# Second feed-forward product by seven block products, in one layer of a streaming encoder on one Trainium2 core

## The chip, the cores and the metric

The kernel runs on one core of a Trainium2 chip. Its engines work side by side: TensorE (PE, with its weight loads shown apart as PEld), VectorE (DVE), ScalarE (ACT), GpSimd (POOL) and SyncE (SP), whose queue issues nearly all DMAs here. The metric is the device time of one execution in microseconds; three runs of the kernel before gave 1771.66, 1764.99 and 1768.73 us, median 1768.73. Everything below about durations is from one profiled execution of it.

## The reference

One layer of a hybrid encoder for 1024 prompt rows and 64 sample rows (1088 columns in the kernel, which holds everything transposed). Projections, sparse attention, a pooling mixer and cross-attention come first and are not touched. The end of the layer is what matters:

```python
def merge_and_ffn(x, ..., w_gate, w_up, w_down):
    ...                                   # x, h = rmsnorm(x, g_ffn)
    return x + (jax.nn.silu(h @ w_gate) * (h @ w_up)) @ w_down
# D_MODEL = 1024, D_FF = 2816 = 22 blocks of 128 rows
```

All of it is in float32. The kernel makes a float32 product from three products of fp32r numbers: each operand is split into a high part (a cast) and a low part (the operand less its high part), and hi x hi, hi x lo and lo x hi are added in PSUM. In what follows "lo" is that second part, computed by one subtraction on VectorE (helper `lo_of`, line 86 of both kernels).

## The kernel before

**Order of the work.** A scheduler orders the instructions of each engine from the program's order and the tiles' dependencies; tiles come from pools with a fixed number of buffers, and an instruction waits until the buffer that it writes has been read for the last time. SP issues DMAs in its own order, so that a DMA whose buffer isn't free holds back those behind it. With `tc.issue_after(x)` a DMA is placed behind x in that order.

**Hidden layer.** The 1088 columns are two sets, 512 and 576 columns (`SETS`), and each is cut into halves of 256 or 288. The 22 row blocks of the hidden layer are worked as 11 pairs p of two blocks. `pair_product` computes one pair for w_gate or w_up: the weights (two loads of 512 KB, L1103) and the normed input are seen as 2 x 2 blocks, and the 2 x 2 product is made from seven block products instead of eight (Strassen-Winograd). For that, sums of weight blocks (`ws`, L1110, three on VectorE, one on GpSimd for each call) and sums of the results (L1141) are needed. Each of the seven has 4 k-blocks x 3 terms of 128x256 or 128x288 products per set (L1127). Weights are cast on ACT (L1119) into a tile of two (`split_tiles`, two buffers) and their lo part is made on VectorE.

`hidden(p, sets)` calls it for w_gate and w_up and then forms u = silu(gate) * up in the tile `tg` (L1186 to L1200), which is stored to DRAM as `u_d[p]` (two blocks of 1088 columns). Pairs 0 and 1 get their first set from `direct` by plain products while the second set's input is still being normed, and only the second set from `hidden`; pairs 2 to 10 get both sets.

**Down stage.** The columns are cut into three chunks (364, 362 and 362). For each chunk eight PSUM banks collect, over the 22 row blocks, 8 output blocks x 3 terms of 128x364 or 128x362 (L1275): 3 x 22 x 24 = 1584 products. For each row block the chunk of u (`uf`, L1266) and 512 KB of w_down (`raw2`, through `wblock`, L110) are loaded, cast on ACT and given lo parts on VectorE, four buffers deep. Then the residual y is added from `yt` (L1279), and the sum is stored (L1280).

Of the kernel before, what the change touches and what calls it, by code (L numbers as in the profile page):

```python
# [45 lines left out]
def encoder_step(ctx: ExitStack, tc: tile.TileContext, a: dict, o: list):  # L46
# [30 lines left out]
    def mm(dt=F32):  # L77
        return psum[0].tile([128, 512], dt, name="mm", tag="mm", bufs=n_mm[0])
# [1017 lines left out]

    def pair_product(name, p, sets, outs, finish):
        raws = []  # L1100
        for e in range(2):
            raw = raw_tile() if (name == "w_up") == (p >= EARLY) else fa.tile([128, 1024], F32, name="fr", tag="fr", bufs=2)
            SP.dma_start(raw.rearrange("p (k j) -> p k j", k=KT), a[name][p + e * NP])  # L1103
# [49 lines left out]
        product(chain, a22, 3, False, True, lambda i: finish(i, t21[i], chain[i]))  # L1153


    def direct(p, between={}):
        n = SETS[0][1]
        h = n // 2
        blocks = [[(HH[0][0][q], HH[0][1][q]) if q is not None else b12_hl for q in qs] for qs in ((0, 1), (None, 2))]
        g = fu.tile([128, 2, n], F32, name="tg", tag="tg", bufs=2)  # L1160
        for name in ("w_gate", "w_up"):
            for e in range(2):
                if (name, e) in between:
                    between[name, e]()
                w = wblock(a[name][p + e * NP], (KT, 128))
                for c in range(2):
                    ps = mm()[:, :h]
                    matmul3(ps, [(w[0][:, k], w[1][:, k], blocks[c][k // 4][0][:, k % 4], blocks[c][k // 4][1][:, k % 4])
                                 for k in range(KT)])
# [5 lines left out]
                if name == "w_up":  # L1175
                    SP.dma_start(u_d[p][e, :, :n], g[:, e])

    def hidden(p, sets):
        def out(i, nm, bufs):
# [10 lines left out]
        pair_product("w_gate", p, sets, g, gate_last)  # L1190
        v = {i: out(i, "tu", 1) for i in sets}

        def up_last(i, t, ps):
            t0, n = SETS[i]
# [7 lines left out]
        pair_product("w_up", p, sets, v, up_last)  # L1202

    EARLY = 2
    turn2, pair_w = [0], []
    u_d = [dram.tile([2, 128, T], F32, name=f"u{p}") for p in range(NP)]
    sq0 = out_proj(0)
    mix_c[1].__exit__(None, None, None)
    hp0_c = tc.tile_pool(name="h0", bufs=1)
# [3 lines left out]

    b12_c = tc.tile_pool(name="b12", bufs=1)
    b12_p = b12_c.__enter__()
    b12_hl = [b12_p.tile([128, 4, 256], F32R, name=f"b12{nm}") for nm in "hl"]

    def first_sums():
        rb = norm_rows(0, *st.pop())
# [32 lines left out]


    fu_c.__exit__(None, None, None)
    for c in (hp1_c, b12_c, fa_c, hp0_c):
        c.__exit__(None, None, None)
    late_c = tc.tile_pool(name="late", bufs=1)
    late = late_c.__enter__()
    for c0, cn in CH:
        acc = [mm()[:, :cn] for f in range(KT)]  # L1260
        for kb in range(NF):
            p, e = kb // 2, kb % 2
            first_kb = c0 == 0 and kb < 2
            up_, nb = (dn, 2) if first_kb else (late, 4)
            uf = up_.tile([128, 364], F32, name="uf", tag="uf", bufs=nb)[:, :cn]
            SP.dma_start(uf, u_d[p][e, :, c0:c0 + cn])  # L1266
            wh, wlo = wblock(a["w_down"][kb], (KT, 128), *(() if first_kb else (
                late.tile([128, 1024], F32, name="raw2", tag="raw2", bufs=4),
                [late.tile([128, 1024], F32R, name=nm, tag=nm, bufs=4) for nm in ("wh2", "wl2")])))
            uh, ul = [up_.tile([128, 364], F32R, name=nm, tag=nm, bufs=nb)[:, :cn] for nm in ("uh", "ul")]  # L1270
            A.copy(uh, uf)
            lo_of(ul, uf, uh)
# [3 lines left out]
        for f in range(KT):  # L1276
            yt = late.tile([128, 364], F32, name="yt", tag="yt", bufs=12)[:, :cn]
            SP.dma_start(yt, y_d[f, :, c0:c0 + cn])
            V.tensor_tensor(yt, acc[f], yt, op=OP.add)  # L1279
            SP.dma_start(o[0][f, :, c0:c0 + cn], yt)  # L1280
    for c in (late_c, dn_c):
        c.__exit__(None, None, None)

# [64 lines left out]
```

## Time and profile before

| what | value |
|---|---|
| median of three runs | 1768.73 us (1764.99 to 1771.66) |
| the profiled execution's own time | 1774.77 us |
| its span | 1772.7 us |
| mean granted clock of TensorE | 0.993 of full speed |
| TensorE busy | 1719.6 us, 97% of the span, 11810 products |
| VectorE, ScalarE, GpSimd busy | 63%, 46%, 23% |
| DMA over the span | 224.26 MB, 127 GB/s |
| hidden layer's products (L1127), idle time before them | 3 x 1120 records, 1.1 us |
| down stage's products (L1275), idle time before them | 3 x 512 records, 0.0 us |

Read the page from its top: which engine is busy nearly all the time, then in which slices, then which lines cost most there and what ended the idle time before them. The duration printed for a product is modelled and contains its pipelining; what one product costs in a stream is read from how many start in a window. A few records of products are missing in the groups of the page, so the counts of the program (1584, for one) are used.

### The profile page before, as it was taken

The numbers are of one execution on the slowest core, as the hardware profiler recorded it, in microseconds if no ns is written. First come the engines' busy times: TensorE is split into PE (matmuls) and PEld (weight loads), VectorE is DVE, ScalarE is ACT, GpSimd is POOL, SyncE is SP. The second block draws the span as 40 slices with busy tenths as digits, with TensorE's granted clock in tenths as the row PEclk, the third lists the DMA queues.
The fourth block names the chain that finished last, engine by engine and source line by source line (L and its number), as shares of the span: only waits on it lengthen the run. The fifth ranks groups of instructions, "written<-read, shape, count | busy, mean of one in ns | idle before, by whom it ended". The sixth has DMA issues, their size and how long they took to land.

```text
span 1772.7 us, 31533 instructions
## 1 busy us (share of the span) xinstructions
PE 1719.6 (97%) x11810; PEld 1668.6 (94%) x11810; DVE 1124.5 (63%) x2411; ACT 813.6 (46%) x1927; POOL 409.5 (23%) x444
## 2 busy tenths in 40 slices
PE   6999999999999998989899999999999999999999
PEld 6999999999999998877798999999999999999999
DVE  6567999999954433778783887544444454544443
ACT  5456677737523432569631354433333333433332
POOL 4111414355412213765203432110000000000000
PEclk9999999999999998999999999999999999999999
DMA  7222441232475336650354333222222221867673
GB/s 231 61 67 73 161 130 46 78 90 98 118 200 190 104 99 207 194 158 1 130 209 137 111 115 130 85 74 74 74 76 89 79 74 43 312 185 244 184 229 98
DMA packets 128582, 224.26 MB, mean 127 GB/s; under 512 B 23463, under 2 KB 86303, under 8 KB 128430
## 3 DMA queue, kind: packets, MB, share of 16 engines
q1 hardware_dynamic: 128430, 222.26, 39.0%
q8 instruction: 93, 1.52, 0.4%
q14 instruction: 59, 0.48, 0.1%
HBM read 167.84 MB, written 54.37 MB: 125 GB/s over the span
## 4 chain that ended last, share of the span: by engine, by line
PE 76%; DVE 11%; ACT 3%; issue 3%; DMA 3%; POOL 2%; SPq 0%; DVEq 0%; ACTq 0%; POOLq 0%
PE mm L1127 24%; PE mm L120 17%; PE mm L1275 15%; PE fl L120 13%; DVE junk_v L780 2%; ACT junk_a L777 2%; PE acc L933 1%; PE tr L903 1%; PE mm L333 1%; DVE wlo L86 1%; PE mm L926 1%; DMA gt<-side_m 1%; DVE lo L86 1%; DVE pl L86 1%; DVE tmlo L86 1%
## 5 line engine op out<-in xcount | busy, mean ns | idle before, releaser
L1127 PE MATMUL mm<-hi,whi 128*128 128x288 f32 (+1 forms) x1120 | 323.2, 289 | 1.1 <-DVE tu L1141 1.1
L1127 PE MATMUL mm<-hi,wlo 128*128 128x288 f32 (+1 forms) x1120 | 324.2, 290 | 0.0
L1127 PE MATMUL mm<-lo,whi 128*128 128x288 f32 (+1 forms) x1120 | 323.5, 289 | 0.0
L1127 PEld LDWEIGHTS mm<-hi,whi 128*128 128x128 f32 x1120 | 211.8, 189 | 1.8 <-DVE tu L1141 1.6
L1127 PEld LDWEIGHTS mm<-lo,whi 128*128 128x128 f32 x1120 | 211.8, 189 | 0.0
L1127 PEld LDWEIGHTS mm<-hi,wlo 128*128 128x128 f32 x1120 | 211.2, 189 | 0.4 <-DVE wlo L86 0.4
L120 PE MATMUL fl<-hh,whi 128*128 128x362 f32 (+1 forms) x576 | 189.7, 330 | 0.9 <-ACT hh L133 0.9
L120 PE MATMUL fl<-hl,whi 128*128 128x362 f32 (+1 forms) x576 | 189.8, 330 | 0.0
L120 PE MATMUL fl<-hh,wlo 128*128 128x362 f32 (+1 forms) x576 | 189.6, 330 | 0.0
L1275 PE MATMUL mm<-uh,wh 128*128 128x362 f32 (+1 forms) x512 | 167.4, 328 | 0.0
L1275 PE MATMUL mm<-ul,wh 128*128 128x362 f32 (+1 forms) x512 | 166.8, 326 | 0.0
L1275 PE MATMUL mm<-uh,wl 128*128 128x362 f32 (+1 forms) x512 | 166.0, 326 | 0.0
L86 DVE TENSOR_TENSOR wl<-raw,wh 128x1024 fp32r<-128x1024 f32 x64 | 78.4, 1225 | 123.4 <-ACT wh L94 123.3
L94 ACT CAST wh<-raw 128x1024 fp32r<-128x1024 f32 x64 | 67.3, 1051 | 145.6 <-PE mm L1275 137.5
L120 PE MATMUL mm<-tmlo,hh 128*128 128x256 f32 (+3 forms) x432 | 122.9, 286 | 1.5 <-DVE tmlo L86 1.5
L120 PE MATMUL mm<-tmhi,hh 128*128 128x256 f32 (+3 forms) x432 | 122.1, 288 | 2.0 <-POOL tmhi L96 2.0
L120 PE MATMUL mm<-tmhi,hl 128*128 128x256 f32 (+3 forms) x432 | 122.6, 286 | 0.0
L86 DVE TENSOR_TENSOR wlo<-raw,whi 128x1024 fp32r<-128x1024 f32 (+1 forms) x75 | 75.9, 1022 | 63.4 <-ACT whi L1119 37.5
L777 ACT ACTIVATE junk_a<-score,cand_a,sgn_a 128x512 f16<-128x512 f32 (+2 forms) x93 | 95.5, 1027 | 42.1 <-DVE cand_a L794 21.8
L120 PEld LDWEIGHTS fl<-hh,whi 128*128 128x128 f32 x576 | 108.3, 188 | 1.7 <-POOL rs L125 1.1
L120 PEld LDWEIGHTS fl<-hl,whi 128*128 128x128 f32 x576 | 108.2, 188 | 0.6
L120 PEld LDWEIGHTS fl<-hh,wlo 128*128 128x128 f32 x576 | 108.2, 188 | 0.5
(386 smaller groups left out, 4545.1 us busy)
## 6 DMA issues: line engine op xcount, KB each, us to landing
raw<-in_w_down_dram SPq DMA_DIRECT2D x66, 512.0 KB, 3.8
fraw<-in_w_gates_dram SPq DMA_DIRECT2D x24, 512.0 KB, 3.7
raw<-in_w_up_dram SPq DMA_DIRECT2D x22, 512.0 KB, 3.8
fr<-in_w_gate_dram SPq DMA_DIRECT2D x18, 512.0 KB, 3.7
side<-side_a SPq DMA_DIRECT2D x8, 1088.0 KB, 6.3
raw<-in_w_out_dram SPq DMA_DIRECT2D x16, 512.0 KB, 3.7
uf<-u SPq DMA_DIRECT2D x44, 181.0 KB, 3.7
u<-tg SPq DMA_DIRECT2D x22, 288.0 KB, 2.1
```

Of the source, the lines that this page charges most:

```text
L86: V.tensor_tensor(lo, src, hi.bitcast(F32), op=OP.subtract)
L94: A.copy(hi, src)
L120: PE.matmul(ps, l, r, start=i == 0, stop=i == n - 1)
L333: PE.matmul(ps[:n, :cn], qt[:, h, :n], kstack[:, k0 + c:k0 + c + cn], start=True, stop=True)
L777: A.activation(junk[:n, :nk], sc, AF.Sign, bias=bj, scale=1.0 if scale is None else scale[:n, j:j + 1], accum_out=sj)
L780: V.tensor_scalar(junk[:n, :nk], sc, bj, None, op0=OP.is_ge, op1=OP.add, accum_out=sj)
L903: PE.matmul(lg[:n, i * 512:i * 512 + cn], qT[:, h, :n], kT[:, kv, s, k0 + c:k0 + c + cn], start=s == 0, stop=s == 1)
L926: PE.transpose(pt[:cn, i * n:(i + 1) * n], probs[i][:, c:c + cn], ident[:n, :n])
L933: PE.matmul(acc, vv, r, start=ji == 0 and i == 0, stop=ji == nj - 1 and i == 1)
L1127: PE.matmul(dst[i], l, r, start=start and j == 0, stop=stop and j == 11, skip_group_check=True)
L1275: PE.matmul(acc[f], l, r, start=kb == 0 and j == 0, stop=kb == NF - 1 and j == 2)
```

## The change

The down product too is now made from seven block products. u of a pair is a row of two blocks, and each of its two column sets has two halves; so u is a 2 x 2 of blocks, and w_down, two row blocks by two halves of the 1024 outputs, another.

- `keep_u` makes the four sums of u that are needed (four subtractions on VectorE per set, L1162), in the tile `tu` of the up product, which is no longer needed then, and stores seven half blocks per pair (L1165 to L1167), 128 x 544 each for both sets. In `hidden` these stores are not issued at once but collected in `later` and issued in the next pair, behind its w_gate loads.
- `down_load` reads a pair's two w_down blocks (2 x 512 KB, L1176), placed behind the w_gate load of a later pair (`SUMS_AT`: pairs 0 and 1 during pair 2, 4 and 5 during pair 5, the others one by one during pairs 3 to 10). `down_sums` makes four sums of 128x512 in place on VectorE (L1181 to L1184), `down_store` stores them (L1188) for products 6, 4, 2 and 5; products 0, 1 and 3 use w_down as it is.
- The down stage runs products 4, 2, 1, 0, 5, 6, 3. Each has 11 blocks (one per pair) of 4 output blocks x 2 column sets x 3 terms of 128x256 and 128x288 (L1343): 7 x 11 x 24 = 1848 products. A block loads 128 x 544 of u and 128 x 512 of weights, eight buffers deep. After a product its eight banks are added into the tile `yl` (L1358), which holds the whole residual and is loaded in 32 parts between the blocks' loads (L1381); after products 0, 5, 6 and 3 the results are stored (L1360). Products 4 and 2 add up in the same banks, and so do products 0, 5, 6 and 3; the list in the diff says which starts or ends a bank. In the last product the blocks of pairs 3 to 10 are held and go bank by bank.

```diff
@@ pair_product
+            ld = SP.dma_start(raw.rearrange("p (k j) -> p k j", k=KT), a[name][p + e * NP])
+        if loaded:
+            loaded(ld.ins)
...
+    def keep_u(i, p, u, t):
+        c0, c1 = UC[i], UC[i + 1]
+        b11, b12, b21, b22 = u[:, 0, 0], u[:, 0, 1], u[:, 1, 0], u[:, 1, 1]
+        for q, x, y_ in ((4, b12, b11), (5, b22, t[:, 1]), (6, b22, b12), (3, b21, t[:, 2])):
+            V.tensor_tensor(t[:, q - 3], x, y_, op=OP.subtract)
+        def store():
+            SP.dma_start(u_d[p][0, :, c0:c1], b11)
+            SP.dma_start(u_d[p][1:3, :, c0:c1].rearrange("q p t -> p q t"), u[:, 1])
+            SP.dma_start(u_d[p][3:7, :, c0:c1].rearrange("q p t -> p q t"), t)
+        return store
+    def down_load(p):
+        pool, tag, n = ((dn, "ud", T), (b12_p, "b12", 1024))[p % 2 == 0]
+        rs = [pool.tile([128, n], F32, name="dr", tag=tag, bufs=2)[:, :1024] for e in range(2)]
+        for e, r in enumerate(rs):
+            SP.dma_start(r.rearrange("p (f j) -> p f j", f=KT), a["w_down"][2 * p + e])
+        return rs
+    def down_sums(r0, r1):
+        a11, a21, a12, a22 = r0[:, :512], r0[:, 512:], r1[:, :512], r1[:, 512:]
+        V.tensor_tensor(a11, a11, a21, op=OP.subtract)
+        V.tensor_tensor(a21, a21, a22, op=OP.add)
+        V.tensor_tensor(a22, a22, a11, op=OP.subtract)
+        V.tensor_tensor(a12, a12, a22, op=OP.subtract)
@@ hidden
+        def loaded(ins):
+            for f in later:
+                f()
+            with tc.issue_after(ins):
+                got.extend((s, down_load(s)) for s in SUMS_AT.get(p, ()))
...
-            SP.dma_start(u_d[p][0, :, t0:t0 + n], gi[:, 0].rearrange("p c t -> p (c t)"))
-            SP.dma_start(u_d[p][1, :, t0:t0 + n], gi[:, 1].rearrange("p c t -> p (c t)"))
+            later.append(keep_u(i, p, gi, vi.rearrange("p e c t -> p (e c) t")))
...
+    SUMS_AT = {2: (0, 1), 3: (2,), 4: (3,), 5: (4, 5), 6: (6,), 7: (7,), 8: (8,), 9: (9,), 10: (10,)}
@@ down stage
-    for c0, cn in CH:
-        acc = [mm()[:, :cn] for f in range(KT)]
-        for kb in range(NF):
...
-            for f in range(KT):
-                for j, (l, r) in enumerate(((wh[:, f], uh), (wh[:, f], ul), (wlo[:, f], uh))):
-                    PE.matmul(acc[f], l, r, start=kb == 0 and j == 0, stop=kb == NF - 1 and j == 2)
...
+    def down_block(q, p):
...
+            raw = late.tile([128, 512], F32, name="raw2", tag="raw2", bufs=8)
+            uf = late.tile([128, T // 2], F32, name="uf", tag="uf", bufs=8)
...
+        last_ld[:] = [SP.dma_start(uf, u_d[p][q]).ins]
...
+    def down_mm(acc, ops, f, i, start, stop):
+        wh, wlo, uh, ul = ops
+        fs, cs = slice(f * 128, f * 128 + 128), slice(UC[i], UC[i + 1])
+        for j, (l, r) in enumerate(((wh, uh), (wh, ul), (wlo, uh))):
+            PE.matmul(acc[f, i], l[:, fs], r[:, cs], start=start and j == 0, stop=stop and j == 2, skip_group_check=True)
...
+    for q, first_, last_, fh, c, done in ((4, True, False, 1, 1, False), (2, False, True, 0, 1, False), (1, True, True, 0, 0, False),
+                                          (0, True, False, 0, 0, True), (5, False, False, 0, 1, True),
+                                          (6, False, False, 1, 1, True), (3, False, True, 1, 0, True)):
...
+            V.tensor_tensor(y, acc[f, i], y, op=OP.add)
+            if done:
+                SP.dma_start(o[0][4 * fh + f, :, s0:s0 + SETS[i][1] // 2], y)
+        together = NP if q != 3 else 3
...
+            if p < together:
+                for f, i in FI:
+                    down_mm(acc, ops, f, i, first_ and p == 0, last_ and p == NP - 1)
+            else:
+                held.append(ops)
+        for f, i in FI:
+            for j, ops in enumerate(held):
+                down_mm(acc, ops, f, i, False, last_ and j == len(held) - 1)
+            evict(f, i)
```

Three places in the instructions' order show how the work moves. The lines of unchanged code are shifted: L1141 becomes L1143, L1110 L1112, L1196, L1198 and L1199 become L1245, L1246 and L1247. First, VectorE between pair 1 and pair 2 before, where `wlo` is a lo part of weights and `ws` a sum of weights:

```order
L1196 TENSOR_TENSOR tg_13144<-tu_13275,tg_13144 128x576
L1141 TENSOR_TENSOR tu_13275<-mm,tu_13275 128x288
L1199 TENSOR_TENSOR tg_13144<-tu_13275,tg_13144 128x288
L86 TENSOR_TENSOR wlo<-fr,whi 128x512
L1110 TENSOR_TENSOR ws<-fr 128x512
L1110 TENSOR_TENSOR ws<-ws,fr 128x512
L1198 TENSOR_TENSOR tg_13144<-mm,tg_13144 128x288
L86 TENSOR_TENSOR wlo<-ws,whi 128x512
```

The same place after; L1162 are the subtractions of u, and L1181 is the first sum of the w_down blocks in `dr`:

```order
L1245 TENSOR_TENSOR tg_13169<-tu_13303,tg_13169 128x576
L1162 TENSOR_TENSOR tu_13303<-tg_13169 128x288
L1143 TENSOR_TENSOR tu_13303<-mm,tu_13303 128x288
L86 TENSOR_TENSOR wlo<-fr,whi 128x512
L1247 TENSOR_TENSOR tg_13169<-tu_13303,tg_13169 128x288
L1112 TENSOR_TENSOR ws<-fr 128x512
L1162 TENSOR_TENSOR tu_13303<-tg_13169,tu_13303 128x288
L1162 TENSOR_TENSOR tu_13303<-tg_13169 128x288
L1112 TENSOR_TENSOR ws<-ws,fr 128x512
L1181 TENSOR_TENSOR dr<-dr 128x512
L1246 TENSOR_TENSOR tg_13169<-mm,tg_13169 128x288
L86 TENSOR_TENSOR wlo<-ws,whi 128x512
```

Between the two lo parts stood three instructions; now there are seven, among them one that waits for a load of w_down. One subtraction also stands ahead of the addition from PSUM.

Second, VectorE in the gate product of pair 5, after; here the sums of two pairs of w_down blocks, pairs 4 and 5, are made:

```order
L86 TENSOR_TENSOR wlo<-ws,whi 128x512 x2
L1182 TENSOR_TENSOR dr<-dr 128x512
L1112 TENSOR_TENSOR ws<-fr 128x512
L1181 TENSOR_TENSOR dr<-dr 128x512
L1183 TENSOR_TENSOR dr<-dr 128x512
L1112 TENSOR_TENSOR ws<-ws,fr 128x512
L1182 TENSOR_TENSOR dr<-dr 128x512
L1184 TENSOR_TENSOR dr<-dr 128x512
L1183 TENSOR_TENSOR dr<-dr 128x512
L86 TENSOR_TENSOR wlo<-ws,whi 128x512 x2
```

Before, only the two sums `ws` stood between these lo parts; six sums of w_down have come between them.

Third, SP at the end of the last pair before, where u_11283 is the last pair's u in DRAM and `uf` and `raw` with a number are the down stage's loads:

```order
L1197 DMA u_11283<-tg_17071 128x576
L1200 DMA u_11283<-tg_17070 128x512
L1266 DMA uf<-u_11274 128x364
L110 DMA raw_17618<-in_w_down_dram 128x1024
L1200 DMA u_11283<-tg_17071 128x576
L1266 DMA uf<-u_11274 128x364
L110 DMA raw_17654<-in_w_down_dram 128x1024
```

The same place after; the stores from `tu` are the sums of u, s_11286 and s_11287 hold stored sums of w_down:

```order
L1166 DMA u_11283<-tg_17275 128x2x256
L1326 DMA uf<-u_11275 128x544
L1332 DMA raw_17839<-s_11286 128x512
L1326 DMA uf<-u_11276 128x544
L1332 DMA raw_17875<-s_11287 128x512
L1167 DMA u_11283<-tu_17519 128x4x256
L1166 DMA u_11283<-tg_17276 128x2x288
L1167 DMA u_11283<-tu_17520 128x4x288
L1381 DMA yl<-y_d 128x256
L1326 DMA uf<-u_11277 128x544
L1332 DMA raw_17921<-s_11288 128x512
```

The loads of the third and fourth block (u_11275 and u_11276) go out ahead of most of the last pair's stores; the fifth block's stand behind three of them.

## Rows read from the trace of the kernel before

**Rows 1.** The page: busy time of the engines, and TensorE in 40 slices

```profile
PE 1719.6 (97%) x11810; PEld 1668.6 (94%) x11810; DVE 1124.5 (63%) x2411; ACT 813.6 (46%) x1927; POOL 409.5 (23%) x444
...
PE   6999999999999998989899999999999999999999
```

**Rows 2.** The page's costliest groups: count, busy us, mean ns, idle before and releaser

```profile
L1127 PE MATMUL mm<-hi,whi 128*128 128x288 f32 (+1 forms) x1120 | 323.2, 289 | 1.1 <-DVE tu L1141 1.1
...
L1275 PE MATMUL mm<-uh,wh 128*128 128x362 f32 (+1 forms) x512 | 167.4, 328 | 0.0
...
L94 ACT CAST wh<-raw 128x1024 fp32r<-128x1024 f32 x64 | 67.3, 1051 | 145.6 <-PE mm L1275 137.5
```

**Rows 3.** Windows: length, busy PE, PEld, DVE, ACT, POOL, PEclk, DMA share, GB/s

```profile
1060.00:1080.00 20.00, 20.00 (x168) 20.00 (x168) 16.11 (x30) 8.14 (x19) 5.23 (x2) 1.00 0.51 164
...
1300.00:1400.00 100.00, 100.00 (x795) 100.00 (x795) 46.83 (x87) 36.29 (x77) 8.37 (x5) 1.00 0.23 76
...
1516.00:1540.00 24.00, 24.00 (x147) 24.00 (x146) 13.12 (x15) 11.46 (x16) 0.00 (x0) 1.00 1.03 382
...
1520.00:1600.00 80.00, 80.00 (x484) 80.00 (x484) 39.28 (x51) 30.09 (x41) 0.00 (x0) 1.00 0.72 240
1600.00:1700.00 100.00, 100.00 (x611) 100.00 (x610) 46.16 (x59) 37.60 (x52) 0.00 (x0) 1.00 0.72 227
```

**Rows 4.** Timeline (start, us): the down stage's first product and its last

```profile
1507.96 0.33 PE L1275 MATMUL mm<-uh,whi 128*128 128x364 f32 x1
...
1768.71 0.32 PE L1275 MATMUL mm<-uh,wl 128*128 128x362 f32 x1
```

**Rows 5.** Timeline: the stores at the end, in SP's queue

```profile
1766.27 3.81 SPq L1280 DMA_DIRECT2D out_dram<-yt  x8
```

**Rows 6.** Timeline: two additions from PSUM in the hidden layer

```profile
1349.24 0.42 DVE L1141 TENSOR_TENSOR tg<-mm,tg 128x256 f32<-128x256 f32 x1 [2.66 <-issue]
1350.83 0.46 DVE L1141 TENSOR_TENSOR tg<-mm,tg 128x288 f32<-128x288 f32 x1 [1.17 <-PE mm L1127]
```

**Rows 7.** Timeline of one pair: weight loads, casts, lo parts; a load's landing

```profile
1346.64 5.71 SPq L1103 DMA_DIRECT2D fr<-in_w_gate_dram  x2
1370.22 1.07 SPq L1103 DMA_DIRECT2D raw<-in_w_up_dram  x2
...
1389.01 5.71 SPq L1103 DMA_DIRECT2D fr<-in_w_gate_dram  x2
...
1356.75 1.14 ACT L1119 CAST whi<-ws 128x512 fp32r<-128x512 f32 x2 [0.42 <-PE mm L1127]
...
1362.80 1.14 ACT L1119 CAST whi<-ws 128x512 fp32r<-128x512 f32 x2 [1.14 <-PE mm L1127]
...
1357.40 1.29 DVE L86 TENSOR_TENSOR wlo<-ws,whi 128x512 fp32r<-128x512 f32 x2
...
1363.45 1.29 DVE L86 TENSOR_TENSOR wlo<-ws,whi 128x512 fp32r<-128x512 f32 x2 [3.43 <-ACT whi L1119]
...
fr<-in_w_gate_dram SPq DMA_DIRECT2D x18, 512.0 KB, 3.7
```

**Rows 8.** Timeline of pairs 0 and 1, and the way to pair 2

```profile
1100.57 0.46 DVE L1141 TENSOR_TENSOR tu<-mm,tu 128x288 f32<-128x288 f32 x1 [0.34 <-PE mm L1127]
...
1101.08 0.40 PE L1127 MATMUL mm<-hi,whi 128*128 128x288 f32 x1 [0.55 <-DVE tu L1141]
...
1126.02 0.69 DVE L86 TENSOR_TENSOR wlo<-fr,whi 128x512 fp32r<-128x512 f32 x1 [1.34 <-ACT whi L1119]
...
1129.30 0.68 DVE L86 TENSOR_TENSOR wlo<-ws,whi 128x512 fp32r<-128x512 f32 x1
```

**Rows 9.** Timeline of the hand-off: block 2's load of u, its casts

```profile
1508.15 0.32 SPq L1266 DMA_DIRECT2D uf<-u  x1
...
1511.39 0.50 ACT L1271 CAST uh<-uf 128x364 fp32r<-128x364 f32 x1 [2.32 <-DMA uf<-u]
1512.59 1.05 ACT L94 CAST wh<-raw 128x1024 fp32r<-128x1024 f32 x1 [0.70 <-DMA raw<-in_w_down_dram]
```

More of the change, by code (lines that the diff above doesn't have):

```diff
@@ L1095, in block_sums, with pair_product @@
             lo_of(b12_hl[1][:, k], b12, b12_hl[0][:, k])
-    def pair_product(name, p, sets, outs, finish):
+    def pair_product(name, p, sets, outs, finish, loaded=None):
         raws = []
@@ L1174, in direct @@
                         V.tensor_tensor(t, ps, t, op=OP.mult)
-                if name == "w_up":
-                    SP.dma_start(u_d[p][e, :, :n], g[:, e])
+        gv = g.rearrange("p e (c t) -> p e c t", c=2)
+        keep_u(0, p, gv, fu.tile([128, 4, h], F32, name="tt", tag="tt", bufs=1))()
     def hidden(p, sets):
@@ L1188, in gate_last @@
             A.activation(g[i][:, 1, 1], g[i][:, 1, 1], AF.Silu)
-        pair_product("w_gate", p, sets, g, gate_last)
+        got = []
+        def loaded(ins):
[3 more added lines that the diff above has]
+                got.extend((s, down_load(s)) for s in SUMS_AT.get(p, ()))
+        pair_product("w_gate", p, sets, g, gate_last, loaded)
+        later.clear()
+        if p == NP - 1:
+            for s, rs in got:
+                down_sums(*rs)
+        for args in sums_of:
+            down_store(*args)
+        sums_of.clear()
         v = {i: out(i, "tu", 1) for i in sets}
         def up_last(i, t, ps):
-            t0, n = SETS[i]
             gi, vi = g[i], v[i]
             V.tensor_tensor(gi[:, 0], vi[:, 0], gi[:, 0], op=OP.mult)
-            SP.dma_start(u_d[p][0, :, t0:t0 + n], gi[:, 0].rearrange("p c t -> p (c t)"))
             V.tensor_tensor(gi[:, 1, 0], ps, gi[:, 1, 0], op=OP.mult)
             V.tensor_tensor(gi[:, 1, 1], vi[:, 1, 1], gi[:, 1, 1], op=OP.mult)
-            SP.dma_start(u_d[p][1, :, t0:t0 + n], gi[:, 1].rearrange("p c t -> p (c t)"))
+            later.append(keep_u(i, p, gi, vi.rearrange("p e c t -> p (e c) t")))
         pair_product("w_up", p, sets, v, up_last)
+        if p < NP - 1:
+            for s, rs in got:
+                down_sums(*rs)
+        sums_of.extend(got)
     EARLY = 2
     turn2, pair_w = [0], []
-    u_d = [dram.tile([2, 128, T], F32, name=f"u{p}") for p in range(NP)]
+    later, sums_of = [], []
+    SUMS_AT = {2: (0, 1), 3: (2,), 4: (3,), 5: (4, 5), 6: (6,), 7: (7,), 8: (8,), 9: (9,), 10: (10,)}
+    UC = (0, SETS[0][1] // 2, T // 2)
+    u_d = [dram.tile([7, 128, T // 2], F32, name=f"u{p}") for p in range(NP)]
+    s_d = [dram.tile([2, 128, 1024], F32, name=f"s{p}") for p in range(NP)]
     sq0 = out_proj(0)
@@ L1215, in encoder_step @@
     b12_p = b12_c.__enter__()
-    b12_hl = [b12_p.tile([128, 4, 256], F32R, name=f"b12{nm}") for nm in "hl"]
+    b12_hl = [b12_p.tile([128, 4, 256], F32R, name=f"b12{nm}", tag="b12", bufs=2) for nm in "hl"]
     def first_sums():
@@ new lines, in encoder_step @@
+    late_c, late = None, None
+    last_ld = []
+    def down_block(q, p):
+        early = late is None
+        if early:
+            raw, uf = raw_tile()[:, :512], fa.tile([128, 1024], F32, name="fr", tag="fr", bufs=2)[:, :T // 2]
+            wh, wlo = [t[:, :512] for t in split_tiles()]
+            ud = dn.tile([128, T], F32R, name="ud", tag="ud", bufs=2)
+            uh, ul = ud[:, :T // 2], ud[:, T // 2:]
+        else:
+            raw = late.tile([128, 512], F32, name="raw2", tag="raw2", bufs=8)
+            uf = late.tile([128, T // 2], F32, name="uf", tag="uf", bufs=8)
+            wh, wlo = [late.tile([128, 512], F32R, name=nm, tag=nm, bufs=8) for nm in ("wh2", "wl2")]
+            uh, ul = [late.tile([128, T // 2], F32R, name=nm, tag=nm, bufs=8) for nm in ("uh2", "ul2")]
+        last_ld[:] = [SP.dma_start(uf, u_d[p][q]).ins]
+        if q in (0, 1, 3):
+            f0 = 4 if q == 3 else 0
+            SP.dma_start(raw.rearrange("p (f j) -> p f j", f=4), a["w_down"][2 * p + (q > 0)][:, f0:f0 + 4])
+        else:
+            e, h = {6: (0, 0), 4: (0, 1), 2: (1, 0), 5: (1, 1)}[q]
+            SP.dma_start(raw, s_d[p][e, :, h * 512:h * 512 + 512])
+        A.copy(wh, raw)
+        lo_of(wlo, raw, wh)
+        A.copy(uh, uf)
+        lo_of(ul, uf, uh)
+        return wh, wlo, uh, ul
```

52 lines of the change are left out of this document (31 added, 21 removed).

## The prediction

> **What bounds the kernel now.** I read the page's busy shares first: TensorE is busy 97% of a span of 1772.7 us, VectorE 63%, and TensorE's slices stand at 9 from the seventeenth of 40 on, which is where the feed-forward part lies [rows 1]. So the end of this kernel is set by how long TensorE's instructions take there, unless something makes it wait. The costliest groups say that it hardly waits: the products of the hidden layer (L1127) have 1.1 us of idle time in 1120 instructions, those of the down stage (L1275) none, and the casts that feed that stage stand idle 137.5 us until a product releases their buffers, so ACT and VectorE run ahead of TensorE by all the buffers they have [rows 2]. The windows by stretch give the pace at a granted clock of 1.00: 795 products in 100 us of the hidden layer (125.8 ns each, half of them 256 columns wide and half 288) and 611 in 100 us of the down stage (163.7 ns, 362 columns) [rows 3]. The down stage runs from 1507.96 us, its first product, to 1768.71, the start of its last [rows 4]: 260.9 us with that one. Behind it come one sum and the last stores, to 1772.7.
>
> **The change, part by part.** *Down stage on TensorE.* Removed: 1584 products, 260.9 us. Added: seven block products of 11 pairs, 4 row blocks, 2 column sets and 3 terms, 1848 products, half of 256 and half of 288 columns. That is the mix of the hidden layer, from the same kind of operands, with additions from PSUM between them as there, so I take its row: 1848 x 125.8 ns = 232.5 us, **-28.4 us**. Bounds: scaled by columns from the down stage's own 163.7 ns a product would take 163.7 x 272 / 363 = 122.7 ns, and the stage 226.7; the other end is that width doesn't count, 163.7 ns for each product, 302.5 us, told below as a rival. Neither has the shapes that are added, the hidden layer's row has.
>
> The rows thus say that 91 columns more cost 37.9 ns more, almost the whole difference in proportion to width. The Trainium skill, "TensorE: Matmul & The Clock Gate", section "Back-to-back issue gap", says otherwise for a stream of weight-load and product pairs: about 81 ns at 128 columns and about 131 at 512, so that much of the cost is fixed per product. By that, read between its two points as an estimate, the 17% more products would eat the narrower ones' gain, 177 us becoming 184, and the forecast would be some 1778 us instead of 1742. The trace disagrees in this kernel, with 163.7 ns at 362 columns.
>
> *Tail.* Before, the eight banks finish half a microsecond apart and their sums and stores crowd the end, 3.8 us of queue work for eight stores [rows 5]. In the last product three blocks go to all banks and the other eight are held, so that a bank finishes every 24 products, 3.0 us. One sum and one store are left: **-0.5 us** (0 to -1.5).
>
> *Feeding the down stage.* A block (24 products, 3.02 us) now needs 256 KB of weights and 272 KB of u, two casts on ACT (1.14 us for two of 512 columns [rows 7], so about 1.2) and two lo subtractions on VectorE (0.69 us each [rows 8], 1.4), and a seventh product adds eight sums of about 0.46 at each turn. All are under half of 3.02 us. Traffic of the stage is 77 x 541 KB + 8.9 MB of residual and output = 50.5 MB in 232.5 us, 217 GB/s; the stage before kept 227 and 240 GB/s in its two first windows with no wait of a product, and 382 from 1516 to 1540 [rows 3]. With eight buffers the operands stand seven blocks, 21 us, ahead. Cost 0. At a turn, bank 0 is complete 2.6 us before the block ends and its sum takes 0.46, so the next product finds it free. If the cover went (the queue at 200 GB/s instead of 217), the stage would be bound by 50.5 MB at 252 us, 20 us later than forecast.
>
> *Hidden layer, pairs 2 to 10.* Added on VectorE per pair: four subtractions of 256 columns and four of 288 (0.42 and 0.46 us [rows 6]), 3.5 us, and four of 512 for the weights' sums (0.69 [rows 8]), 2.8 us: 6.3 us on about 19.8 of the 42.4 us of a pair (46.8 per 100 [rows 3]; a pair's length is the distance of its gate loads, 1346.64 to 1389.01 [rows 7]). Nine pairs hold 57 us of it, and it lies beside TensorE: a pair of weight blocks is cast when TensorE releases its tile, at 1356.75 and again at 1362.80; the lo parts of the first are done at 1358.69 and wanted at 1362.80, so 4.1 us are free in each 6.05 [rows 7]. At the tightest place (pair 5, two pairs of sums) six of the eight sums, 4.1 us, stand ahead of two lo parts that had 3.4 us of idle time before them, so 0.7 of the 4.1 us is used. Cost 0, up to 1 us a pair in which they bunch. The sums' loads follow the second gate load (at about 1352) in SP's queue; landing takes 3.7 us as the gate loads' [rows 7], 1356 to 1357, just as the sum's turn comes. Stores of the sums stand ahead of the w_up loads, which wait until 1370.22 for their tiles anyway; the sums are through by then.
>
> *Pairs 0 and 1* run one set and have no such slack. In each, a subtraction of 0.46 us comes before an addition that had 0.34 us of idle time and for which TensorE already stood 0.55 us [rows 8]: 0.12 us each, **+0.2**. *The way from pair 1 to 2*: before, VectorE waited 1.34 us there, then did without a pause what TensorE waited for, until the lo at 1129.30 [rows 8]. Now two subtractions and the first sum, 1.6 us, and an L1247 that slid behind a lo come in between, some of it into the 1.34: **+0.9**, at least 0 and at most 3, if the four new loads of 512 KB, issued right behind the gate's two, land late. *Direct pairs*: eight subtractions of 0.42, less two lo subtractions of u that went; VectorE is busy 16.1 of 20 us there [rows 3]: **+0.5** (0 to 1.5).
>
> *Hand-off to the down stage.* Blocks 0 and 1 are loaded early, 6.05 us of work; before, two blocks were 8.0 us. Block 2's first load was issued at 1508.15, its u was cast from 1511.39 and its weights from 1512.59 [rows 9]; now the weights are half as long, cast by 1512.6, lo by 1513.4, wanted at 1507.96 + 6.05 = 1514.0. Blocks 4 on are queued behind 1.4 MB of stores of u: 3.1 MB since 1508 at 382 GB/s land at 1516.2, wanted at 1520.1. **+0.5** (0 to 6, the last at 230 GB/s).
>
> Sum: -28.4 - 0.5 + 0.2 + 0.9 + 0.5 + 0.5 = **-26.8 us**. The rows' run took 1774.77 us and would take 1748.0. It lies 6.0 us over the median of 1768.73 without any stretch that I could name for it, so I take the difference from the median: 1741.9, **1742 us**.
>
> **Rivals.**
> 1. *A part given back where cover is thin* (the hand-off, the early pairs, a bunch of subtractions in each pair). For it: the hand-off's margin of 0.6 us, and VectorE's queue in order. Against: 4.1 us in each weight window. With 6 us at the hand-off, 3 at the way to pair 2, 1.5 at the direct pairs and 0.5 in each of nine pairs, 15 us of costs in place of 2.1: 1755. The usual size would be half of that, 1746 to 1755.
> 2. *The down stage is bound by its transfers.* At 200 GB/s 252 us: 1762, no gain worth naming below it. Against: 227 to 240 GB/s were kept for 180 us without a wait, and the new stage moves less in all than the old (50.5 MB for 55.8).
> 3. *Slower: the sums' wait in VectorE's queue.* Place: the first sum of each of nine pairs, which waits for its load, with PSUM additions and the lo parts of the next weights behind it, and TensorE behind these. It decides from 27 / 9 = 3 us of waiting TensorE per pair; with 4.1 us of slack the load would have to land some 7 us after the sum's turn, 10 or more after its issue. At 4.5 us a pair, 40 us: 1782. Against: gate loads of the same size land in 3.7 us, and the stage moves 76 GB/s [rows 3], about 140 with the new traffic.
> 4. *Slower: a product's spacing doesn't follow its width.* From 141 ns a product the stage is no shorter than before; at 163.7 ns the time is 1768.7 + 41.6 + 2.1 = 1812. Against: the hidden layer's 125.8 ns for the same shapes. It is the mechanism of the section cited above.
>
> **Chances and range.** The forecast case, 1738 to 1746, has 0.68; the first rival 0.23; the second 0.05; the third 0.03; the fourth 0.01. The range is 1737 to 1754 us, down to a tail and costs at their best and up to nearly all of rival 1; what is left out is about 0.15. This kernel's runs differ by about 0.4%, so 0.5%, 8.8 us, is what can be told from no change: faster (under 1759.9) holds the first two cases and a third of rival 2, 0.93; within 0.5% most of rival 2, 0.03; slower rivals 3 and 4, 0.04.
>
> **What would show it.** In the profile after: L1343 with 1848 products (924 of each width) at 125 to 127 ns by the windows, and idle time near 0 in its groups; the last product of the hidden layer no more than 3 us later than 1507.83; VectorE at about 62% in the hidden layer's windows; pairs still 42.4 us apart by their gate loads. Wrong if pairs are longer (sums in VectorE's way), if L1343's groups show idle time behind a DMA or behind a lo, or if the first 20 us of the stage hold a gap of several microseconds.

## The result, and the profile after

The changed kernel takes 1749.43 us (median of four runs, 1745.08 to 1752.41) against 1768.93 us (1764.99 to 1771.66): a ratio of 0.989, 95% interval 0.986 to 0.992, 19.5 us less. Measured again, in the last comparison below, it is 0.9896 (0.9878 to 0.9914). The forecast was 26.8 us less. The time lies inside the range of 1737 to 1754 us but outside the likeliest case, 1738 to 1746; it is the first rival, a part given back where cover is thin.

The page of the profiled execution after (1747.69 us, span 1745.9), for [rows 1, 2]; columns as there:

```profile
span 1745.9 us, 32493 instructions
...
PE 1688.0 (97%) x12074; PEld 1637.8 (94%) x12074; DVE 1179.2 (68%) x2597; ACT 810.8 (46%) x1949; POOL 412.4 (24%) x444
...
L1129 PE MATMUL mm<-hi,whi 128*128 128x288 f32 (+1 forms) x1120 | 323.7, 290 | 5.7 <-ACT whi L1121 4.3
...
L1343 PE MATMUL mm<-uh,wh 128*128 128x256 f32 (+1 forms) x600 | 169.2, 290 | 2.1 <-ACT wh L1333 2.1
```

TensorE has 264 products more and 31.6 us less to do. But its products wait longer than before: in these two groups 5.7 us in the hidden layer (1.1 before) and 2.1 in the down stage (none before).

**A trap in the spans.** They differ by 1772.7 - 1745.9 = 26.8 us, to the tenth the forecast, and that proves nothing. The first product of the hidden layer starts at 1079.50 us before and at 1072.83 after: 6.7 us of the difference arose ahead of that product. The 384 products just ahead of it, nearly all of the direct pairs, take 46.49 us in both kernels, so it arose earlier still, in code that the change doesn't touch; in the other profiled runs below this start lies anywhere from 1067.6 to 1079.7. So I compare stretches between products that both kernels have, by their starts in the timeline. The hidden layer has 3360 products; A is from the first to the 49th (four block products of pair 0), B from there to the 401st (pairs 0 and 1 and the way to pair 2), C from there to the last; D is from the down stage's first product to the start of its last:

| kernel | A | B | C | D | A to D |
|---|---|---|---|---|---|
| before | 6.48 | 48.63 | 373.21 | 260.75 | 689.21 |
| after | 9.41 | 51.37 | 373.20 | 235.51 | 669.62 |
| difference | +2.93 | +2.74 | -0.01 | -25.24 | -19.59 |

With the tail (from the start of the last product to the end of the span 3.99 us before, 3.45 after) that is 20.1 us, close to the 19.5 of the medians. A, B and D hold all of it but the tail's half microsecond. How the losses divide among the three differs from run to run, as the table at the end of the experiments shows.

Windows after, for [rows 3]: length, busy PE, PEld, DVE, ACT, POOL, PEclk, DMA share, GB/s:

```profile
1300.00:1400.00 100.00, 100.00 (x795) 100.00 (x794) 57.29 (x113) 37.06 (x78) 8.37 (x5) 1.00 0.44 151
...
1540.00:1600.00 60.00, 60.00 (x481) 60.00 (x481) 34.83 (x61) 26.02 (x44) 0.00 (x0) 1.00 0.89 298
1600.00:1700.00 100.00, 100.00 (x800) 100.00 (x799) 52.08 (x91) 38.67 (x66) 0.00 (x0) 1.00 0.66 202
```

In the hidden layer the number of products in 100 us is unchanged, 795, with VectorE at 57 where it was at 47 and the traffic doubled. In the down stage 800 products lie in 100 us, some 125 ns each.

**Where the three losses are.** Stretch A, timeline (start, us; in brackets the idle time before and what ended it):

```profile
1075.65 0.37 SPq L1167 DMA_DIRECT2D u<-tt  x1
...
1076.13 0.62 ACT L1121 CAST whi<-ws 128x512 fp32r<-128x512 f32 x1 [2.04 <-issue]
...
1078.76 0.40 ACT L1145 COPY tg<-mm 128x288 f32<-128x288 f32 x1 [1.49 <-DVE wlo L86]
...
1077.32 0.40 PE L1129 MATMUL mm<-hi,whi 128*128 128x288 f32 x1 [1.14 <-ACT whi L1121]
...
1079.21 0.40 PE L1129 MATMUL mm<-hi,whi 128*128 128x288 f32 x1 [1.36 <-ACT tg L1145]
```

The third block product goes on in the bank of the first, which ACT's copy must have read. Before, that copy started 2.75 us after the hidden layer's first product, now 5.93. Its tile is the first of a pool that takes the place of the direct pairs' pool, whose last store had just landed, at 1078.58: u<-tt, where `tt` is the tile of that pool into which the direct pairs put their sums. The same copy before, and a cast that followed it there:

```profile
1082.25 0.40 ACT L1143 COPY tg<-mm 128x288 f32<-128x288 f32 x1 [1.48 <-DMA u<-tg]
...
1083.36 0.62 ACT L1119 CAST whi<-raw 128x512 fp32r<-128x512 f32 x1
```

The order has changed here too. Before, the twelve products of the third block come first; after, two of the sixth stand ahead of them (1077.32), and ACT casts the sixth's weights ahead of the copy. That alone would put the copy at 4.4 us at the earliest and A at 7.9 (an estimate: the end of the cast, 1077.26, and the 3.48 us from the copy's start to the 49th product). The store landed later than that, so in this run the store decides.

Stretch B, the way from pair 1 to pair 2, in the same form; below it the windows of two of those microseconds:

```profile
1116.53 0.89 SPq L1103 DMA_DIRECT2D fr<-in_w_gate_dram  x2
...
1119.71 0.29 PE L1129 MATMUL mm<-hi,wlo 128*128 128x288 f32 x1
1122.64 0.58 PE L1129 MATMUL mm<-hi,whi 128*128 128x256 f32 x1 [2.63 <-ACT whi L1121]
...
1121.97 0.62 ACT L1121 CAST whi<-fr 128x512 fp32r<-128x512 f32 x1 [5.42 <-DMA fr<-in_w_gate_dram]
...
1123.00:1124.00 1.00, 1.00 (x6) 1.00 (x6) 1.00 (x3) 0.00 (x0) 0.72 (x1) 0.50 1.06 369
1124.00:1125.00 1.00, 1.00 (x6) 1.00 (x6) 1.00 (x1) 0.00 (x0) 0.82 (x1) 0.50 0.97 360
```

The product that waits is 256 columns wide, so it is pair 2's (pairs 0 and 1 have 288 alone). TensorE's order has changed: before, all 336 products of pairs 0 and 1 came first; now two of pair 2 stand behind the 324th, and they wait for weights issued at 1116.53. After the wait the granted clock is 0.50, the lower level, for some 3 us.

The hand-off to the down stage (first product 1506.94):

```profile
1507.99 2.36 SPq L1326 DMA_DIRECT2D uf<-u  x1
...
1510.92 0.38 SPq L1167 DMA_DIRECT2D u<-tu  x1
1511.39 0.45 SPq L1166 DMA_DIRECT2D u<-tg  x1
1511.94 1.22 SPq L1167 DMA_DIRECT2D u<-tu  x1
1513.21 1.34 SPq L1381 DMA_DIRECT2D yl<-y_d  x1
1514.61 1.14 SPq L1326 DMA_DIRECT2D uf<-u  x1
...
1519.48 0.65 ACT L1335 CAST uh<-uf 128x544 fp32r<-128x544 f32 x1 [5.09 <-DMA uf<-u]
...
1521.32 2.11 PE L1343 MATMUL mm<-uh,wh 128*128 128x256 f32 x8 [2.09 <-ACT wh L1333]
...
1522.00:1523.00 1.00, 1.00 (x7) 1.00 (x6) 0.19 (x1) 0.84 (x2) 0.00 (x0) 0.50 1.04 399
```

The fifth block's load of u (1514.61) stands in SP's queue behind the last pair's three stores and one load of the residual. TensorE is through with four blocks at 1519.23, waits 2.09 us, and then runs at half clock, 0.50.

### The profile page after: what moved, and what is told of

Its sections match the earlier page's. It is cut to its first block, busy times and chain, and to the rows that moved or that the text cites. A ratio compares the mean times of both kernels' runs of the same rounds, so it can differ in the third digit from the quotient of the medians.

```text
span 1745.9 us, 32493 instructions
## 1 busy us (share of the span) xinstructions
PE 1688.0 (97%) x12074; PEld 1637.8 (94%) x12074; DVE 1179.2 (68%) x2597; ACT 810.8 (46%) x1949; POOL 412.4 (24%) x444
## 4 chain that ended last, share of the span: by engine, by line
PE 59%; DVE 7%; DMA 3%; issue 2%; ACT 1%; POOL 1%; SPq 0%; DVEq 0%; ACTq 0%; POOLq 0%
PE mm L1129 24%; PE mm L1343 13%; PE mm L120 9%; PE fl L120 8%; PE acc L933 1%; PE tr L903 1%; DVE lo L86 1%; DVE wlo L86 1%; PE mm L926 1%; DVE fr L1083 1%; DVE ws L1090 0%; PE mm L615 0%; POOL ws L1090 0%; DVE pl L86 0%; DVE pr L907 0%
## 5 line engine op out<-in xcount | busy, mean ns | idle before, releaser
L1343 PE MATMUL mm<-uh,wh 128*128 128x256 f32 (+1 forms) x600 | 169.2, 290 | 2.1 <-ACT wh L1333 2.1
L1343 PE MATMUL mm<-ul,wh 128*128 128x256 f32 (+1 forms) x600 | 169.5, 289 | 0.0
L1343 PE MATMUL mm<-uh,wl 128*128 128x256 f32 (+1 forms) x600 | 167.6, 288 | 0.0
L1343 PEld LDWEIGHTS mm<-uh,wh 128*128 128x128 f32 x600 | 111.9, 190 | 2.4 <-ACT wh L1333 2.3
L1343 PEld LDWEIGHTS mm<-ul,wh 128*128 128x128 f32 x600 | 112.4, 190 | 0.0
L1343 PEld LDWEIGHTS mm<-uh,wl 128*128 128x128 f32 x600 | 111.2, 188 | 0.0
```

The lines of the kernel that those rows point to most:

```text
L1343: PE.matmul(acc[f, i], l[:, fs], r[:, cs], start=start and j == 0, stop=stop and j == 2, skip_group_check=True)
```

## Experiments

Ten runs follow: nine edited kernels, and the changed kernel once more. Stretches in us; what is not named is as after. The first four were made to undo one loss each.

**a_gp**: the direct pairs' subtractions on another engine.

```diff
-        keep_u(0, p, gv, fu.tile([128, 4, h], F32, name="tt", tag="tt", bufs=1))()
+        keep_u(0, p, gv, fu.tile([128, 4, h], F32, name="tt", tag="tt", bufs=1), G)()
```

> The four subtractions of u of each direct pair go from VectorE to GpSimd; nothing else changes. Measure: from the hidden layer's first product (pair 0) to its 49th, 6.48 us before and 9.40 us after. Theory (three subtractions in VectorE's queue hold back the lo parts of the first weights): 6.5 us, and the rest of the feed-forward part as after (from the 49th to the 401st product 51.4 us, down stage 235.5 us from first to last start). Rival (the loss comes from the stores and loads that run there, not from VectorE's queue): it stays at 9.4 us.

Measured: A 13.59, far from the theory's 6.5 and from the rival's 9.4. Timeline of this kernel:

```profile
1083.70 0.37 SPq L1167 DMA_DIRECT2D u<-tt  x1
...
1086.72 0.40 ACT L1145 COPY tg<-mm 128x288 f32<-128x288 f32 x1 [4.70 <-DMA u<-tt]
...
1082.50 1.17 POOL L1162 TENSOR_TENSOR tt<-tg,tt 128x256 f32<-128x256 f32 x1
...
1081.88 1.21 DVE L1112 TENSOR_TENSOR ws<-ws,fr 128x512 f32<-128x512 f32 x1
...
1085.48 0.61 PE L1129 MATMUL mm<-hi,wlo 128*128 128x288 f32 x1 [2.87 <-DVE wlo L86]
```

GpSimd takes 1.04 to 1.18 us for each where VectorE takes 0.42, so the store goes out later, and here the copy is put down to that store. But TensorE did not wait for this copy. In this kernel's order all twelve products of the sixth block come first, and the wait of 2.87 us inside them was ended by a lo part on VectorE, behind two sums of weights that took 1.21 and 1.09 us where the same sums took 0.69 after. Then some 24 products ran 0.24 us apart, at half clock. So VectorE lost four subtractions and yet was later, and a_gp doesn't tell the queue of VectorE from the store. The row of the copy gave a new theory, tested by two kernels. In **a_none** the second direct pair's sums are not computed:

```diff
-            V.tensor_tensor(t[:, q - 3], x, y_, op=OP.subtract)
+            if (i, p) != (0, 1):
+                V.tensor_tensor(t[:, q - 3], x, y_, op=OP.subtract)
...
+            if (i, p) != (0, 1):
+                for pp in (p, 1)[:2 if (i, p) == (0, 0) else 1]:
+                    SP.dma_start(u_d[pp][3:7, :, c0:c1].rearrange("q p t -> p q t"), t)
```

> The four subtractions of u of the second direct pair, and their store of 512 KB, are left out (those of the first direct pair are stored in their place, so pair 1's sums for set 0 are not computed). Measure: from the hidden layer's first product to its 49th, 6.48 us before, 9.41 after, 13.59 with the subtractions on GpSimd. New theory for that loss (the subtractions' time is not the point: ACT's first copy from PSUM into the new pool's tile waits until the last store out of the pool that it replaces has landed, and the third block product waits for the copy; so the loss follows the landing of the store): 6.5 to 7.2 us. Rival (subtractions between the lo parts of the first weights, or loads): 8.5 us or more.

In **a_split** their store is cut in four:

```diff
+            if i == 0 and p == 1:
+                for q in (4, 5, 6, 3):
+                    SP.dma_start(u_d[p][q, :, c0:c1], t[:, q - 3])
+            else:
+                SP.dma_start(u_d[p][3:7, :, c0:c1].rearrange("q p t -> p q t"), t)
```

> The store of the second direct pair's four sums (512 KB) is issued as four of 128 KB, each when its sum is there; all else as after. Same measure, 9.41 us after. Theory (landing of the last store): the last one is a quarter as long and lands about 1 us sooner, 8.0 to 8.8 us. Rival (another cause): 9.4 us or more.

Measured: A 6.93 and 8.77, both in the theory's ranges. Neither settles it alone: a_none takes out the subtractions together with the store, and 8.77 is only 0.2 under the lowest of the kernels with this code as it is (8.97, below). The copy in a_none and in a_split:

```profile
1070.82 0.40 ACT L1145 COPY tg<-mm 128x288 f32<-128x288 f32 x1 [1.93 <-DMA u<-tg]
...
1083.20 0.40 ACT L1145 COPY tg<-mm 128x288 f32<-128x288 f32 x1 [0.85 <-DMA u<-tt]
```

What tells the store from the rest is the copy's start. In all twelve profiled executions (before and every kernel here) it lies 0.07 to 0.25 us behind the landing of the last store of the old pool. In the seven where the profile names VectorE's lo part instead, as after, that part ended within 0.01 us of the copy's start, in five of them behind it, so the copy can't have waited for it. The store itself goes out 0.03 us after VectorE's last subtraction, so VectorE's queue matters through it.

From the copy's start to the 49th product it is 3.48 us in after, b_shift, c_late and a_split, and 3.73 in before, a_none and best. In the last two TensorE's and ACT's order is again that of before, so they gained by the order as well as by the store. Among the seven kernels with this code as it is, the copy starts 5.49 to 6.94 us after the first product, and A is 8.97 to 11.94. In four of them (b_gp, b_gp_shift, d_more, after2) 1.3 to 1.5 us of A come from the clock, which fell for some 14 products behind the wait, as here in after2:

```profile
1084.00:1085.00 1.00, 1.00 (x6) 1.00 (x6) 0.00 (x0) 0.30 (x1) 0.00 (x0) 0.50 0.57 229
```

The profiled run after, with 9.41 and no such fall, was a mild one.

**b_shift** and **b_gp** divide the loss between pair 1 and pair 2.

```diff
-    SUMS_AT = {2: (0, 1), 3: (2,), 4: (3,), 5: (4, 5), 6: (6,)
+    SUMS_AT = {3: (0, 1), 4: (2, 3), 5: (4, 5), 6: (6,)
```

> The loads and sums of w_down of pairs 0 and 1 go from pair 2 to pair 3, and those of pair 2 to pair 4, so that at the way from pair 1 to pair 2 no load of w_down and no sum is left. Measure: from the 49th to the 401st product of the hidden layer, 48.64 us before and 51.38 us after. Theory (TensorE's order: the first product of pair 2 now stands ahead of the last block product of pair 1 and waits for its weights' load, and the clock falls in that wait): no change, 51.4 us within 0.5. Rival (the forecast's own term: four loads of 512 KB and a sum in VectorE's queue): 49.5 us or less.

```diff
-            later.append(keep_u(i, p, gi, vi.rearrange("p e c t -> p (e c) t")))
+            later.append(keep_u(i, p, gi, vi.rearrange("p e c t -> p (e c) t"), G if p < EARLY else V))
```

> The four subtractions of u of the hidden layer's pairs 0 and 1 go to GpSimd; loads and sums of w_down stay in pair 2. That also puts TensorE's order back: all 336 products of pairs 0 and 1 stand ahead of pair 2's first. Measure: from the 49th to the 401st product, 48.64 us before and 51.38 after. Theory (TensorE's order): 48.6 to 49.4 us. Rival (loads and sums of w_down): 51 us or more.

Measured: B 51.80 with the loads and sums moved, 49.97 with TensorE's order put back. The first row is b_shift's, still waiting at pair 2's first product; the others are b_gp's, which has the wait of [rows 8] again and another one within pair 2:

```profile
1129.23 0.50 PE L1129 MATMUL mm<-hi,whi 128*128 128x256 f32 x1 [2.80 <-ACT whi L1121]
...
1121.81 0.40 PE L1129 MATMUL mm<-hi,whi 128*128 128x288 f32 x1 [0.55 <-DVE tu L1143]
...
1129.16 0.39 PE L1129 MATMUL mm<-hi,wlo 128*128 128x256 f32 x1 [0.67 <-DVE wlo L86]
```

The wait for pair 2's weights goes with the order: in all eight profiled kernels with the new order TensorE is idle 1.88 to 2.89 us at that product, and in the three with the old one (b_gp, b_gp_shift, best) 0.55 us at the old place. What b_gp can't separate is the order from the subtractions, whose move to GpSimd put it back. And 49.97 is neither the 48.6 to 49.4 of the theory nor the 51 of the rival: the wait of 0.67 us for a lo part suggests that something of the forecast's own term, the sums in VectorE's queue, is left. **b_gp_shift** does both:

> Subtractions of pairs 0 and 1 on GpSimd and, besides, the loads and sums of w_down of pairs 0 and 1 in pair 3, those of pair 2 in pair 4. Measure: from the 49th to the 401st product, 48.63 us before, 51.37 after, 51.80 with the loads and sums moved alone, 49.97 with GpSimd alone. If the way to pair 2 loses by both (TensorE's order first, and with that put right 1.3 us by the sums in VectorE's queue): 48.6 to 49.0 us. Rival (order alone, and the 1.3 us is GpSimd's or the stores'): 49.7 us or more.

Measured: B 48.86, below all eight kernels with the new order (49.82 to 51.90). So order and sums together make the loss. How much each costs is less sure. Between b_gp and b_gp_shift, one run each, the loads and sums make 1.1 us. But seven kernels with the same code in this stretch lie 2.1 us apart: 49.82 and 50.65 where the clock did not fall (a_none, c_late), 51.37 to 51.90 where it did. The subtractions on VectorE show nothing of their own at the end of pair 0: the product that waits there starts 0.87 us behind the one before it, 0.84 in the kernel before.

**c_late**: the last pair's stores further back in the queue.

```diff
-            if q == 4 and p == 3:
+            if q == 4 and p == 6:
                 for f in later:
                     f()
+            if q == 4 and p == 3:
                 for args in sums_of:
```

> The last pair's three remaining stores of u (1.4 MB) are issued behind the loads of the down stage's seventh block instead of the fourth's. Measure: from the down stage's first product to the start of its last, 235.51 us after. Theory (the fifth block's loads stand behind the stores in SP's queue, TensorE waits 2.2 us and then runs some 3 us at half clock): 232.7 us within 0.5, no wait over 0.3 us in the first 20 us of the stage. Rival (the first loads are limited by the rate of the transfers or by the time SP takes to issue them, with or without stores): 234.5 us or more.

Measured: D 231.46, no product of the stage later than 0.2 us after the one before it. Over the 20 us around the hand-off, at 319 GB/s:

```profile
1504.00:1524.00 20.00, 20.00 (x162) 20.00 (x161) 10.64 (x19) 7.79 (x13) 0.00 (x0) 1.00 0.96 319
```

That is 0.7 us below the theory's range and far from the rival's 234.5: the stores' place in the queue was the cause, and it cost more than expected. 231.46 is the stage without a wait: 125.3 ns a product. It also gives the size of the loss after: 4.05 us, of which 2.2 are the wait and the rest the lower clock. In the other runs with this code the same wait cost 0.7 to 2.1 us, without a fall of the clock.

**d_more**: how much VectorE has left in the hidden layer.

```diff
+        for j in range(extra):
+            V.tensor_tensor(a12, a12, a22, op=OP.subtract if j % 2 else OP.add)
...
-                down_sums(*rs)
+                down_sums(*rs, {6: 4, 7: 8, 8: 12, 9: 16}.get(p, 0))
```

> In pairs 6, 7, 8 and 9 the sums of w_down are followed by 4, 8, 12 and 16 more operations of 128x512 on VectorE (added and taken off again), 2.8, 5.5, 8.3 and 11.0 us each. Measure: the length of each pair, 42.37 us in all nine pairs before and after. Theory (each 6.05 us weight window leaves VectorE some 4 us, over seven windows a pair): up to 8 more operations cost nothing, 12 nothing or under 0.5 us, 16 up to 2 us. Rival (the stores of the sums stand ahead of the w_up loads in SP's queue, so that late sums hold the loads): 1 us or more from 8 operations on.

Measured: every pair 42.37 or 42.38 us long. The sums run ahead of the pair that they are named for, so that the fullest two pairs of TensorE's time are these:

```profile
1338.91:1381.28 42.37, 42.37 (x338) 42.37 (x337) 33.21 (x62) 15.19 (x32) 3.34 (x2) 1.00 0.42 146
1381.28:1423.65 42.37, 42.37 (x338) 42.37 (x337) 33.36 (x62) 15.19 (x32) 3.35 (x2) 1.00 0.39 131
```

At 79% of a pair, where the change has 60% (25.5 of 42.4), VectorE still holds nobody up. The added operations spread over several pairs, at most 7.8 us more in one, so the 11.0 us in one pair that the expectation speaks of were not tried, and the limit was not reached.

**best**, all remedies together, and **after2**, the changed kernel again, in the same five rounds. Beside the edits of b_gp_shift and c_late, the second direct pair's u is stored as it is and loaded back in pair 0:

```diff
+                if name == "w_up" and p == 1:
+                    SP.dma_start(ug[e], g[:, e])
...
+            back, sums = [fu.tile([128, 2, 2, 256], F32, name=n_, tag=n_, bufs=b_) for n_, b_ in (("tg0", 2), ("tu0", 1))]
+            SP.dma_start(back.rearrange("p e c t -> p e (c t)"), ug.rearrange("e p t -> p e t"))
+            later.append(keep_u(0, 1, back, sums.rearrange("p e c t -> p (e c) t"), G))
```

> All remedies at once: the second direct pair's u is stored as it is, loaded back during pair 0 and its four sums made on GpSimd; the subtractions of pairs 0 and 1 on GpSimd; loads and sums of w_down of pairs 0 to 2 moved to pairs 3 and 4; the last pair's stores behind the seventh block's loads. By the parts measured alone: hidden layer from its first to its 49th product 6.9 us (6.48 before, 9.41 after), to the 401st 48.9 (48.63, 51.37), the rest 373.2, down stage 231.5 (260.75, 235.51); from the first hidden product to the last down product 660.7 us against 689.2 before and 669.6 after, so 1740 us where before takes 1769, 8 to 10 us less than after. Rival (what one wait gives back another takes, since each run's stalls lie at other places): 665 us or more.

> The changed kernel again, unchanged, for its time beside the kernel before on the same chip: 1749 us, a ratio of 0.989. From the first hidden product to the last down product 667 to 672 us, by how long the store lands that the first copy waits for and whether the clock falls at the hand-off.

| kernel | A | B | C | D | A to D |
|---|---|---|---|---|---|
| after2 | 11.94 | 51.90 | 373.20 | 232.62 | 669.80 |
| a_gp | 13.59 | 51.43 | 373.20 | 233.57 | 671.92 |
| a_none | 6.93 | 49.82 | 373.20 | 232.86 | 662.94 |
| a_split | 8.77 | 51.66 | 373.20 | 232.22 | 665.99 |
| b_shift | 8.97 | 51.80 | 373.21 | 233.40 | 667.51 |
| b_gp | 11.65 | 49.97 | 373.21 | 232.50 | 667.46 |
| b_gp_shift | 11.69 | 48.86 | 373.21 | 233.03 | 666.92 |
| c_late | 10.06 | 50.65 | 373.20 | 231.46 | 665.50 |
| d_more | 11.39 | 51.89 | 373.21 | 232.13 | 668.76 |
| best | 7.30 | 49.03 | 373.21 | 231.46 | 661.13 |

Best takes 1738.55 us (1733.65 to 1743.36) where before takes 1765.09 and after2 1748.77: a ratio to before of 0.9849 (0.9825 to 0.9874), clear of after2's 0.9896 (0.9878 to 0.9914). Its 661.13 us from A to D were expected as 660.7, after2's 669.80 as 667 to 672. Beside before it still loses 0.8 us in A and 0.4 in B.

## Why the prediction was right or wrong

The direction and the range held; the size was too large by 7 us, and the likeliest case was the wrong one of the two that share the range. To take the difference from the median was sound: the start of the hidden layer lies 12 us apart among the profiled runs, and the kernel before was profiled with one of the latest. One row was misread without harm: TensorE's slices stand at 9 from the twenty-first on, not the seventeenth, and the feed-forward part begins later still. Term by term, in the profiled run:

- **Down stage on TensorE, -28.4.** Right: without a wait the stage is 29.3 us shorter (260.75 to 231.46), 125.3 ns a product where [rows 3] gave 125.8. The fourth rival, a spacing that ignores width, is out, and with it the estimate by the Trainium skill's "TensorE: Matmul & The Clock Gate", "Back-to-back issue gap": 17% more products cost little beyond their columns, 125.3 ns each where the scaling by columns gave 122.7. (The paces read from windows are a little short, since a window also counts the products cut by its ends: by starts, 126.1 ns in a pair's 42.37 us and 164.7 in the old down stage.)
- **Feeding it, 0, and the turns.** Right: in none of the eleven profiled runs of the new stage does a product start over 0.3 us behind the one before it after the first 15 us. The second rival is out; after, the windows hold 298 and 202 GB/s with TensorE always busy.
- **Hidden layer, pairs 2 to 10, 0.** Right to the hundredth (C 373.21 and 373.20), and by d_more with room to spare. The third rival never came near.
- **Tail, -0.5.** Right: 0.54.
- **Pairs 0 and 1, +0.2.** Too high: 0.03 at pair 0, and pair 1's is part of the way to pair 2.
- **Direct pairs, +0.5 (0 to 1.5).** The step that failed most, beyond its upper bound. I priced eight subtractions as VectorE's time; the direct pairs' own products took no longer for them (46.49 us before and after). What they did is to delay a store that a pool's turnover waits for, and the copy in the new pool, and the third block product: +2.9 here, 2.5 to 5.5 in other runs of the same code, of which up to 1.5 is the clock. The wait was there before, 1.48 us long at ACT's first copy, and cost nothing because it ended just in time.
- **The way from pair 1 to 2, +0.9.** Right in kind, wrong in place: I had counted VectorE's queue and not looked at TensorE's own order, where two products of pair 2 had moved ahead of twelve of pair 1. +2.7. The term that I had named, sums and loads, is about 1.1 once the order is put right, by one run each.
- **Hand-off, +0.5 (0 to 6).** The place and the mechanism were named (blocks from the fifth on behind the stores) but sized too small: I took the queue to issue at once, and the transfers to run at 382 GB/s, to land at 1516.2. They ran at 277, and the fifth block's load went out at 1514.61 and its cast began at 1519.48. The issue of one load alone held SP for 2.36 us; in after2 and b_shift, where it took 0.42, the fifth block's load went out 6.4 us after the stage's first product, here 7.7. The loss is 4.05 here, 0.7 to 2.1 in others. The window in question:

```profile
1508.00:1519.40 11.40, 11.24 (x89) 10.90 (x87) 3.75 (x7) 2.50 (x4) 0.00 (x0) 1.00 0.89 277
```

Together -29.3 + 0.0 - 0.5 + 0.0 + 2.9 + 2.7 + 4.05 = -20.1. That this run comes so near the 19.5 of the medians is in part luck: after2 has nearly the same sum, 669.80 us from A to D, with losses of 5.5, 3.3 and 1.2 us in place of 2.9, 2.7 and 4.05.

The first rival had all this as "hand-off, way to pair 2, direct pairs" and a usual size of 1746 to 1755. What should have raised its chance above 0.23 is that three places without cover were known, each with an upper bound, and that I took each near its lower end; the direct pairs' bound was itself too low.

## What to carry to other kernels

Work that is spread under a busy engine can be free in the steady state and be paid at the seams: price each change of stage by what its first instruction waits for (a pool's last store, a queue's position), not by the busy time of the engine that does the work. Read the new order of the bottleneck engine itself at each seam; here two products ahead of twelve meant a wait of 1.9 to 2.9 us, while the work that was added under nine pairs cost nothing. And compare stretches between instructions that both kernels share before believing a difference of spans.

## What the runs showed of the hardware that was not expected

- The granted clock fell to its lower level after a wait of TensorE in some runs and not in others: after (2.63 us idle, then 0.50 for 3 us) and c_late (2.82 us idle at the same place, clock 1.00 throughout, in the row below). A fall cost 1.3 to 1.8 us more than the wait, in stretch A of four runs and at the hand-off in after.
```profile
1122.00:1123.00 1.00, 1.00 (x9) 1.00 (x9) 1.00 (x3) 0.00 (x0) 0.76 (x1) 1.00 1.02 406
```

- A VectorE operation of 128x512 took 1.21 us beside GpSimd's subtractions in a_gp, 0.69 without. The Trainium skill, "SBUF — State Buffer", section "SBUF: two separate sides", says that a VectorE operation with two inputs in SBUF and a GpSimd operation that reads SBUF exclude each other on a shared port; the 0.52 us more agree with that in kind.
- In the feed-forward part after, the issue of one DMA held SP for 0.33 us in the median and for 2.36 us at the most; that longest one was a load issued 1.05 us after the down stage's first product, and the same load took 0.42 us in c_late and after2.
